# z and six LRU gate projections moved from whole units to seven-product pairs, with the SSD rows, the LRU states and the group norm

## The chip, the cores and the metric

The kernel runs on one core of a Trainium2 chip. It is written by hand for the core's engines: TensorE (PE) multiplies, VectorE (DVE), ScalarE (ACT) and GpSimd (POOL) work on elements, SyncE (SP) issues DMAs; POOL and ACT issue DMAs too. Each engine takes its own instructions in the order of the program and waits on semaphores for the others. The metric is the device time of one execution in microseconds, lower is better; the runs give a median.

## The reference

One decoder layer with 1024 tokens and width 1024 in float32. `xn` is the RMS norm of the input, and one projection of it feeds three mixers and three merge gates. Cut to what matters here:

```
proj = hn @ w_in                                   # u, v | xb, gate | z | x,B,C | dt | g0, g1, g2
yb = gelu(gate) * lru_scan(conv(xb))               # 8 blocks of 128 channels
y  = ssd(conv(x,B,C), dt) + x * d_skip             # 4 groups of 256 channels
y  = y * silu(z)
yg = y.reshape(.., 4 groups, 256)
yc = yg * rsqrt(mean(yg * yg, -1) + EPS) * norm_g  # the group norm
gates  = sigmoid(g + b_gate)
merged = sum over branches: gates[k] * (y_k @ w_branch_k)
h = x + merged @ w_out;  h = h + (relu(rms(h) @ W1) ** 2) @ W2;  out = rms(h)
```

Each product is done to nearly float32 accuracy from a high and a low part of both operands: high x high, high x low, low x high, three matmuls in place of one.

## The kernel before

A matmul is 128 x 128 weights by 512 columns. The program has these stages: the input norm and the projection v (to about 140 us), the **unit stage** (to 770 us), the **pair stage** (to about 1005 us), the branch merge, the output projection, and the MLP.

*Unit stage.* A unit is 128 output channels for all 1024 tokens: 8 slices of the input x 3 x 2 halves of tokens = 48 matmuls (`product`, L555) into a PSUM tile `ps` of which there are two. Then its `post` runs: a conv (L576, L578), a gelu (`gelu2`, L235 to L238) or a gate. `queue` holds the units in order: for each SSD group r B, C, x0, x1, z0, z1, then for two LRU heads the conv input `xb` and the gate; after that eight gMLP units. There are 48 in all: 8 for z, 8 for LRU gates, 16 for the rest of SSD, 8 for `xb`, 8 for gMLP. Work that belongs to finished units stands in generators in `pending`. `step` (after each unit) moves each one on by a `yield`. For SSD these are `ssd_stages`: `s1_` builds decays and C B products, `s2_` the states, `s3_` the rows y (L738 to L740), which it multiplies by the gated z (L741) and squares (L743); `s4_` does the group norm (L749 to L759): a matmul with a matrix of ones sums over the channels, ACT takes the root, and DVE makes and corrects the reciprocal. For an LRU head, `stages` does the two small gate products (L816), the scan (L831) and the product with the gelu gate. Results go to DRAM as `yb_d`, `yc_d`, `ya_d`. In this stage a scheduler sets the order of the engines' rows.

*Pair stage.* A pair is 256 output channels. Instead of 96 matmuls for two units it takes 84: a Strassen-like form with seven products of 12 matmuls each (`seventh`, L478), of sums and differences of blocks of the weights (A11, A12, A22, S1 to S4) and of `xn` (B11, B21, B22, T1 to T4, made once by `x_forms`). Twelve pairs make the three merge gates. The order is written out by hand (`manual_schedule`): p1 of a pair, p4 of the pair before, then p2, p5, p6, p3, p7. Behind each product stands what frees its PSUM tile, and between them the preparation of the next pair's weights: `cast1`, `sums1`, `sums2`, `cast12`, `cast22`, and `cast34` of this pair. A cast is `split`: ACT makes the high part (L132), DVE the low part (L133). p1, p6, p7 and p4 accumulate into one PSUM tile `b1`: p6 waits until ACT has copied what p1 left there (L934), p7 until ACT has copied that of p6 (L950), and p4 until DVE has added that of p7 (L958) to its partner. p5 and p3 share `b2` in the same way (L945, L954).

Of the kernel before, what the change touches and what calls it, by code (L numbers as in the profile page):

```python
# [36 lines left out]
def trunk_kernel(ctx: ExitStack, tc: tile.TileContext, x, norm_mix_g, w_in, b_gate, gmlp_ln_g, gmlp_ln_b,  # L37
# [23 lines left out]
    mixers = ExitStack()  # L61
    halfp = mixers.enter_context(tc.tile_pool(name="half", bufs=16))
    lrup = mixers.enter_context(tc.tile_pool(name="lruw", bufs=1))
    const = mixers.enter_context(tc.tile_pool(name="const", bufs=1))
# [139 lines left out]
    def columns(name, rws, n):  # L204
        ps = aux()
        nc.tensor.transpose(out=ps[:, :n], in_=rws[:n, :P], identity=ident[:n, :n])
        cols = const.tile([P, n], F32, name=name)
        nc.vector.tensor_copy(out=cols, in_=ps[:, :n])
        return cols
# [75 lines left out]
    with tc.manual_schedule():  # L285
# [21 lines left out]
        ones = const.tile([P, P], F32, name="ones")  # L307
# [115 lines left out]
    va = columns("va", acs, P)  # L423
# [157 lines left out]
    gd = [dram.tile([KD, P, T], F32, name=f"g{b}_d") for b in range(3)]  # L581

# [39 lines left out]
    def ssd_units(g):  # L622
        S = {}

        def xbc(key, ct):
            def post(ps):
                c = act()
                conv(c, ps, [scw[:, j * 16 + ct:j * 16 + ct + 1] for j in range(4)], vh[:, SCB + ct:SCB + ct + 1])
                t = act()
                actv(t, c, AF.Tanh)  # L630
                stt(out=c, in0=t, scalar=1.0, in1=c, op0=ALU.add, op1=ALU.mult)
# [5 lines left out]
        def z(j):  # L637
            def post(ps):
                t = act()
                actv(t, ps, AF.Tanh, scale=0.5)  # L640
                stt(out=t, in0=t, scalar=1.0, in1=ps, op0=ALU.add, op1=ALU.mult)
                S["z", j] = t
            unit_in(C_Z + (2 * g + j) * P, post)

        xbc("b", 8 + g)
        xbc("c", 12 + g)
        xbc("x0", 2 * g)
        xbc("x1", 2 * g + 1)
        z(0)
        z(1)  # L650

    def ssd_stages(g, S):
# [3 lines left out]
        xdt, xw, E, cb, pv, er, sq = {}, {}, {}, {}, {}, {}, {}  # L656
# [68 lines left out]
        def s3_(half):  # L725
            tk = hsl(half)
            for j in range(2):
# [9 lines left out]
                Z = S["z", j]  # L737
# [3 lines left out]
                tt(out=Z[:, tk], in0=y, in1=Z[:, tk], op=ALU.mult)  # L741
                sq[half, j] = half_()
                actv(sq[half, j], Z[:, tk], AF.Square)  # L743
            nc.gpsimd.tensor_tensor(out=sq[half, 0], in0=sq[half, 0], in1=sq[half, 1], op=ALU.add)

        def s4_(half):
            tk = hsl(half)
            vs = aux()
            mm(vs, ones, sq[half, 0], start=True, stop=True)  # L749
            r, q = half_(), half_()  # L750
            actv(r, vs, AF.Sqrt, scale=1.0 / 256, bias=eps4)
            nc.vector.reciprocal(out=r, in_=r)  # L752
            tt(out=q, in0=r, in1=r, op=ALU.mult)
            stt(out=q, in0=vs, scalar=256 * 4.0 * EPS, in1=q, op0=ALU.add, op1=ALU.mult)
            ts(out=q, in0=q, scalar1=-0.5 / 256, scalar2=1.5, op0=ALU.mult, op1=ALU.add)
            tt(out=r, in0=r, in1=q, op=ALU.mult)
            for j in range(2):
                Z = S["z", j]
                stt(out=Z[:, tk], in0=Z[:, tk], scalar=va[:, SNG + 2 * g + j:SNG + 2 * g + j + 1], in1=r, op0=ALU.mult, op1=ALU.mult)  # L759
                nc.gpsimd.dma_start(out=yd["c"][2 * g + j][:, tk], in_=Z[:, tk])  # L760

# [10 lines left out]
        s4_(0)  # L772
# [3 lines left out]
        yield  # L776
        s3_(1)
        yield
        yield
        s4_(1)  # L780


    def lru_units(h):
        S = {}

        def post_x(ps):
# [8 lines left out]
            for half in range(2):  # L795
                p_ = half_(dt=F32R), half_(dt=F32R)
                split(p_[0], p_[1], xb[:, hsl(half)])
                S["xs"].append(p_)

        def post_g(ps):  # L800
            S["g2"] = act()
            gelu2(S["g2"], ps, T)
            later(stages())
            if h == 7:
                v_group(0)

        def stages():
# [25 lines left out]
            nc.gpsimd.tensor_tensor(out=S["g2"], in0=y, in1=S["g2"], op=ALU.mult)  # L833
            nc.gpsimd.dma_start(out=yd["b"][h], in_=S["g2"])
            yield

        unit_in(C_XB + h * P, post_x)
        unit_in(C_GATE + h * P, post_g)
# [80 lines left out]
    class GatePair:  # L919
        def __init__(self, br, e):  # L920
            self.br, self.e = br, e
            self.w = Weights(w_in, C_G + br * D + e * P, w4)
# [4 lines left out]
        def gate(self, o, src, b):  # L927
            actv(o, src, AF.Tanh, scale=0.5, bias=vh[:, BG + self.br * 8 + self.e + b:BG + self.br * 8 + self.e + b + 1])

        def p1(self):  # L930
            self.b1 = gps.tile([P, HF], F32, tag="gps", name=nm("gps"))
            self.mul(self.b1, "A11", "B11", True)
            self.o0 = act()
            actv(self.o0[:, hsl(0)], self.b1, AF.Copy)  # L934

        def p2(self):
            b0 = gps.tile([P, HF], F32, tag="gps", name=nm("gps"))
            self.mul(b0, "A12", "B21", True)
            tt(out=self.o0[:, hsl(0)], in0=b0, in1=self.o0[:, hsl(0)], op=ALU.add)

        def p5(self):
            self.b2 = aux()
            self.mul(self.b2, "S1", "T1", True)
            self.o1 = act()
            actv(self.o1[:, hsl(1)], self.b2, AF.Copy)  # L945
            self.gate(self.o0[:, hsl(0)], self.o0[:, hsl(0)], 0)

        def p6(self):
            self.mul(self.b1, "S2", "T2", False)
            actv(self.o0[:, hsl(1)], self.b1, AF.Copy)  # L950

        def p3(self):
            self.mul(self.b2, "S4", "B22", False)
            tt(out=self.o0[:, hsl(1)], in0=self.b2, in1=self.o0[:, hsl(1)], op=ALU.add)  # L954

        def p7(self):
            self.mul(self.b1, "S3", "T3", False)
            tt(out=self.o1[:, hsl(1)], in0=self.b1, in1=self.o1[:, hsl(1)], op=ALU.add)  # L958
            self.gate(self.o0[:, hsl(1)], self.o0[:, hsl(1)], 0)
            nc.gpsimd.dma_start(out=gd[self.br][self.e], in_=self.o0)  # L960

        def p4(self):
            self.mul(self.b1, "A22", "T4", False)
            self.gate(self.o1[:, hsl(0)], self.b1, 1)
            self.gate(self.o1[:, hsl(1)], self.o1[:, hsl(1)], 1)
            nc.gpsimd.dma_start(out=gd[self.br][self.e + 1], in_=self.o1)

    pairs = [(br, e) for br in (1, 0, 2) for e in range(0, KD, 2)]
    cur = []

    def first_pair():
        z = GatePair(*pairs.pop(0))
# [8 lines left out]

    for r in range(4):
        ssd_units(r)
        lru_units(2 * r)
        lru_units(2 * r + 1)
# [39 lines left out]
    two = (P, 2, HF)  # L1025
# [196 lines left out]

    z, prev = cur.pop(), None
    with tc.manual_schedule():
        z.w.cast22()
        while z:
            nxt = GatePair(*pairs.pop(0)) if pairs else None
# [31 lines left out]
            prev, z = z, nxt  # L1259
    for n in list(XF):  # L1260
# [529 lines left out]
```

## Time and profile before

| | us |
|---|---|
| runs, median of 3 | 1985.93 (1985.53 to 1985.93) |
| the profiled execution | 1988.2 |
| its span, first to last instruction | 1986.5 |
| PE / DVE / ACT / POOL busy | 1929.9 / 1340.0 / 988.2 / 313.6 |
| granted PE clock, mean | 0.987 |

The page's costliest groups are matmuls. Its columns are line, engine, operation, output and inputs, shape and count, then busy time and the mean of one in ns, then the idle time of the engine before them and what ended it. Here the two groups of the units and one of the pair stage:

```profile
L555 PE MATMUL ps<-xn,wh 128*128 128x512 f32 x1536 | 418.4, 392 | 0.0
...
L555 PE MATMUL ps<-xn,wl 128*128 128x512 f32 x768 | 236.7, 389 | 0.0
...
L478 PE MATMUL gps<-xn,wt 128*128 128x512 f32 x432 | 102.2, 389 | 2.1 <-DVE a L238 2.1
```

1536 + 768 = 2304 matmuls are the 48 units. The 389 ns are the time through the array; the next matmul starts sooner, so the rate is read from the start times.

### The profile page before, as it was taken

The numbers are of one execution on the slowest core, as the hardware profiler recorded it, in microseconds if no ns is written. First come the engines' busy times: TensorE is split into PE (matmuls) and PEld (weight loads), VectorE is DVE, ScalarE is ACT, GpSimd is POOL, SyncE is SP. The second block draws the span as 40 slices with busy tenths as digits, with TensorE's granted clock in tenths as the row PEclk, the third lists the DMA queues.
The fourth block names the chain that finished last, engine by engine and source line by source line (L and its number), as shares of the span: only waits on it lengthen the run. The fifth ranks groups of instructions, "written<-read, shape, count | busy, mean of one in ns | idle before, by whom it ended". The sixth has DMA issues, their size and how long they took to land.

```text
span 1986.5 us, 23821 instructions
## 1 busy us (share of the span) xinstructions
PE 1929.9 (97%) x9012; PEld 1607.3 (81%) x9012; DVE 1340.0 (67%) x1917; ACT 988.2 (50%) x1431; POOL 313.6 (16%) x406
## 2 busy tenths in 40 slices
PE   8999999999999998999999999998999999999996
PEld 7998878788788787888888888777788887888885
DVE  5485666875866688444477888247665657788787
ACT  6425665756756643444354544166555555243243
POOL 4112222232322443000010110000111110000000
PEclk8999999999999999999999999999999999999998
DMA  4256547457366473333398986331544358543532
GB/s 160 59 147 137 116 106 156 94 117 143 92 133 130 107 191 106 117 117 106 122 277 273 267 219 177 138 106 54 178 156 164 128 184 299 174 154 123 190 115 88
DMA packets 207208, 293.93 MB, mean 148 GB/s; under 512 B 12804, under 2 KB 125652, under 8 KB 207092
## 3 DMA queue, kind: packets, MB, share of 16 engines
q1 hardware_dynamic: 163540, 151.20, 24.7%
q0 software_dynamic: 34544, 119.69, 23.5%
q10 hardware_dynamic: 9008, 21.51, 3.1%
q8 instruction: 71, 1.16, 0.2%
q14 instruction: 45, 0.37, 0.1%
HBM read 188.41 MB, written 67.24 MB: 129 GB/s over the span
## 4 chain that ended last, share of the span: by engine, by line
PE 80%; DVE 11%; ACT 4%; issue 3%; DMA 2%; POOL 1%; SPq 0%; ACTq 0%; DVEq 0%; POOLq 0%
PE aux L478 39%; PE ps L555 22%; PE gps L478 8%; PE aux L257 4%; PE aux L1312 2%; PE aux L816 1%; PE aux L735 1%; PE aux L731 1%; DVE a L578 1%; ACT a L1361 1%; DVE a L831 1%; DVE h L752 1%; DVE rsq_q L111 1%; DVE a L133 1%; DVE a L702 1%
## 5 line engine op out<-in xcount | busy, mean ns | idle before, releaser
L555 PE MATMUL ps<-xn,wh 128*128 128x512 f32 x1536 | 418.4, 392 | 0.0
L555 PEld LDWEIGHTS ps<-xn,wh 128*128 128x128 f32 x1536 | 286.8, 188 | 61.2 <-issue 2.8
L478 PE MATMUL aux<-b,b 128*128 128x512 f32 x1152 | 263.9, 389 | 0.1
L478 PEld LDWEIGHTS aux<-b,b 128*128 128x128 f32 x1152 | 216.1, 188 | 45.3 <-DVE b L133 0.5
L555 PE MATMUL ps<-xn,wl 128*128 128x512 f32 x768 | 236.7, 389 | 0.0
L478 PE MATMUL aux<-a,b 128*128 128x512 f32 x960 | 219.4, 389 | 0.0
L478 PEld LDWEIGHTS aux<-a,b 128*128 128x128 f32 x960 | 180.2, 188 | 37.4
L555 PEld LDWEIGHTS ps<-xn,wl 128*128 128x128 f32 x768 | 144.1, 188 | 30.3
L478 PE MATMUL aux<-b,wt 128*128 128x512 f32 x672 | 156.9, 389 | 0.0
L478 PEld LDWEIGHTS aux<-b,wt 128*128 128x128 f32 x672 | 126.1, 188 | 26.2
L132 ACT ACTIVATE b<-wt 128x1024 fp32r<-128x1024 f32 x88 | 90.7, 1053 | 83.8 <-DMA wt<-u_d 58.8
L133 DVE TENSOR_TENSOR b<-wt,b 128x1024 fp32r<-128x1024 f32 x88 | 107.2, 1219 | 17.3 <-ACT b L132 17.3
L133 DVE TENSOR_TENSOR wt<-a,wt 128x1024 fp32r<-128x1024 f32 x52 | 63.7, 1225 | 73.1 <-ACT wt L132 73.1
L1542 DVE TENSOR_TENSOR a<-aux,a 128x512 f32<-128x512 f32 x112 | 77.0, 688 | 50.5 <-PE aux L478 50.4
L478 PE MATMUL gps<-xn,wt 128*128 128x512 f32 x432 | 102.2, 389 | 2.1 <-DVE a L238 2.1
L526 ACT ACTIVATE wh<-raw 128x1024 fp32r<-128x1024 f32 x48 | 50.7, 1056 | 104.3 <-PE ps L555 99.2
L478 PEld LDWEIGHTS gps<-xn,wt 128*128 128x128 f32 x432 | 80.9, 188 | 19.2 <-issue 2.5
L133 DVE TENSOR_TENSOR a<-a,a 128x1024 fp32r<-128x1024 f32 (+1 forms) x61 | 61.8, 1020 | 38.9 <-ACT a L132 38.8
L478 PE MATMUL aux<-a,wt 128*128 128x512 f32 x336 | 81.6, 400 | 3.4 <-ACT a L1419 3.4
L578 DVE SCALAR_TENSOR_TENSOR a<-ps,scw,a 128x1023 f32<-128x1023 f32 (+2 forms) x48 | 61.1, 1273 | 33.3 <-ACT a L576 32.5
L528 POOL DMA_DIRECT2D wl<-raw x48 | 42.9, 893 | 248.5 <-ACT wl L527 88.3
L478 PEld LDWEIGHTS aux<-a,wt 128*128 128x128 f32 x336 | 65.0, 194 | 18.0 <-ACT a L1419 4.2
(339 smaller groups left out, 3372.2 us busy)
## 6 DMA issues: line engine op xcount, KB each, us to landing
wt<-u_d SPq DMA_DIRECT2D x54, 512.0 KB
raw<-in_w_in_dram SPq DMA_DIRECT2D x48, 512.0 KB
wl<-raw POOLq DMA_DIRECT2D x48, 512.0 KB, 5.0
u_d<-a POOLq DMA_DIRECT2D x48, 512.0 KB, 5.2
g_d<-a POOLq DMA_DIRECT2D x24, 512.0 KB, 2.9
a<-g_d ACTq DMA_DIRECT2D x24, 512.0 KB
rt<-in_w_mlp_up_dram SPq DMA_DIRECT2D x17, 512.0 KB
a<-acs_d POOLq DMA_DIRECT2D x32, 256.0 KB, 8.0
```

The source lines that it names most:

```text
L111: stt(out=q, in0=r, scalar=nh, in1=r, op0=ALU.mult, op1=ALU.mult)
L132: actv(dst_hi, src, AF.Copy)
L133: (eng or nc.vector).tensor_tensor(out=dst_lo, in0=src, in1=dst_hi.bitcast(F32), op=ALU.subtract)
L257: mm(ps[:, :nt], X.tok(a, k, c), wk[k][w], start=(k == 0 and i == 0), stop=(k == KD - 1 and i == 2))
L478: mm(ps, lhs[l][kk], rhs[r][kk], start=(new and n == 0), stop=(n == 11), skip_group_check=not new)
L526: actv(hi, raw, AF.Copy)
L528: nc.gpsimd.dma_start(out=lo, in_=raw, accum_op=ALU.add)
L555: mm(ps[:, hsl(h)], w[wi][:, k, :], a.rhs(ai, k, h), start=(n == 0), stop=(n == 3 * KD - 1))
L578: stt(out=dst[:, j:], in0=ps[:, :T - j], scalar=taps[3 - j], in1=dst[:, j:], op0=ALU.mult, op1=ALU.add)
L702: tt(out=e[:, cc], in0=e[:, cc], in1=cbm[:, i].unsqueeze(1).to_broadcast([P, 4, P]), op=ALU.mult)
L1312: mm(ps, M.tok(a, k, c), wo[nb][k][w], start=(k == 0 and a + w == 0), stop=(k == KD - 1 and a == 1))
L1542: tt(out=h, in0=ps, in1=h, op=ALU.add)
```

## The change

- z (8 blocks) and six of the eight LRU gate blocks leave the unit list: 14 units fewer. They become seven pairs among the twelve gate pairs: kind "z" (4 pairs), "g" (3) and "t" (the gates as before). The heads 6 and 7 keep their gate units.
- The LRU heads are spread 2, 2, 1, 3 over the four SSD groups.
- `s3_` stores its rows y to DRAM (`yr_d`) and is done; `s4_` goes away. Heads 0 to 5 store their states (`hr_d`); their stages start one step later.
- A z or g pair reads the rows back (`rows`, in two halves, from SP) and hands its half to a generator: `post_g` is the gelu and the product, `post_z` the gate, the product, and the whole group norm. The main loop calls `step` seven times per pair.
- The order of the branches among the gate pairs changes, and the two halves of a gate pair are stored by half of the tokens, not by block.
- `ones` and `va` move to the lasting pool; the vectors' pool is closed before the pair stage, and four tiles `actx` take its place.

```diff
@@ ssd_units, ssd_stages
-        z(0)
-        z(1)
...
                 stt(out=y, in0=Xf[j][:, tk], scalar=dcol[:, 2 * g + j:2 * g + j + 1], in1=y, op0=ALU.mult, op1=ALU.add)
-                tt(out=Z[:, tk], in0=y, in1=Z[:, tk], op=ALU.mult)
-                sq[half, j] = half_()
-                actv(sq[half, j], Z[:, tk], AF.Square)
-            nc.gpsimd.tensor_tensor(out=sq[half, 0], in0=sq[half, 0], in1=sq[half, 1], op=ALU.add)
-
-        def s4_(half):
...
+                nc.gpsimd.dma_start(out=yr_d[2 * g + j][:, tk], in_=y)
...
@@ lru_units
+            if h < PLAIN:
+                later(stages(False))
...
+            if gated:
+                nc.gpsimd.tensor_tensor(out=S["g2"], in0=y, in1=S["g2"], op=ALU.mult)
+                nc.gpsimd.dma_start(out=yd["b"][h], in_=S["g2"])
+            else:
+                nc.gpsimd.dma_start(out=hr_d[h], in_=y)
...
-        unit_in(C_GATE + h * P, post_g)
+        if h >= PLAIN:
+            unit_in(C_GATE + h * P, post_g)
...
-    class GatePair:
+    class Pair:
+        def rows(self, half):
+            if self.kind != "t":
+                self.y[half] = actx()
+                nc.sync.dma_start(out=self.y[half], in_=self.part({"z": yr_d, "g": hr_d}[self.kind], half))
+
+        def done(self, half):
+            if self.kind == "t":
+                nc.gpsimd.dma_start(out=self.part(gd[self.br], half), in_=self.o[half])
+            else:
+                later({"z": self.post_z, "g": self.post_g}[self.kind](half))
+
+        def post_g(self, half):
+            o, y, t = self.o[half], self.y[half], actx()
+            actv(t, o, AF.Square)
+            stt(out=t, in0=t, scalar=1.0 / GELU_C, in1=o, op0=ALU.add, op1=ALU.mult)
+            actv(t, t, AF.Tanh, scale=GELU_S * GELU_C)
+            yield
+            stt(out=o, in0=t, scalar=1.0, in1=o, op0=ALU.add, op1=ALU.mult)
+            tt(out=o, in0=o, in1=y, op=ALU.mult)
+            nc.gpsimd.dma_start(out=self.part(yd["b"], half), in_=o)
+
+        def post_z(self, half):
+            o, y, t = self.o[half], self.y[half], actx()
+            actv(t, o, AF.Tanh, scale=0.5)
+            stt(out=o, in0=t, scalar=1.0, in1=o, op0=ALU.add, op1=ALU.mult)
+            tt(out=o, in0=o, in1=y, op=ALU.mult)
+            actv(t, o, AF.Square)
+            yield
+            tt(out=t[:, 0], in0=t[:, 0], in1=t[:, 1], op=ALU.add)
+            yield
+            yield
+            vs = aux()
+            mm(vs, ones, t[:, 0], start=True, stop=True)
+            r, q = y[:, 0], y[:, 1]
+            actv(r, vs, AF.Sqrt, scale=1.0 / 256, bias=eps4)
+            nc.vector.reciprocal(out=r, in_=r)
+            tt(out=q, in0=r, in1=r, op=ALU.mult)
+            stt(out=q, in0=vs, scalar=256 * 4.0 * EPS, in1=q, op0=ALU.add, op1=ALU.mult)
+            ts(out=q, in0=q, scalar1=-0.5 / 256, scalar2=1.5, op0=ALU.mult, op1=ALU.add)
+            tt(out=r, in0=r, in1=q, op=ALU.mult)
+            for b in range(2):
+                col = SNG + self.e + b
+                stt(out=o[:, b], in0=o[:, b], scalar=va[:, col:col + 1], in1=r, op0=ALU.mult, op1=ALU.mult)
+            nc.gpsimd.dma_start(out=self.part(yd["c"], half), in_=o)
...
+    for i in range(3):
+        pairs.insert(5 * i + 1, ("z", 0, 2 * i))
+        pairs.insert(5 * i + 3, ("g", 0, 2 * i))
+    pairs.insert(15, ("z", 0, 6))
...
+    for r, heads in enumerate(((0, 1), (2, 3), (4,), (5, 6, 7))):
...
@@ main loop of the pair stage
             z.p1()
             z.w.cast34()
+            step()
             if prev:
                 prev.p4()
+                step()
             z.p2()
...
+            step()
             z.p5()
...
+            step()
             z.p6()
...
+            step()
             z.p3()
...
+            step()
             z.p7()
...
+            step()
             prev, z = z, nxt
```

The 19 pairs now come in the order t z t g t t z t g t t z t g t z t t t: behind each z and each g pair stands a gate pair.

How the change moves instructions is seen in the order of the built programs. On DVE, before, between the low parts of the next pair's first weights (L133, `wt`) and p7's add (L958) stand the weight sums (L502 to L507), a cast, p3's add (L954) and a cast:

```order
L133 TENSOR_TENSOR wt_6506<-rt_6468,wt_6505 128x1024
L502 TENSOR_TENSOR a_6525<-a_6469 128x512
L503 TENSOR_TENSOR a_6526<-rt_6468,a_6469 128x512
L506 TENSOR_TENSOR a_6525<-a_6525,rt_6468 128x512
L507 TENSOR_TENSOR a_6526<-rt_6468,a_6525 128x512
L133 TENSOR_TENSOR wt_6545<-a_6525,wt_6544 128x1024
L954 TENSOR_TENSOR a_6485<-aux_6509,a_6485 128x512
L133 TENSOR_TENSOR a_6561<-a_6469,a_6561 128x512
L958 TENSOR_TENSOR a_6522<-gps_6472,a_6522 128x512
```

After, in the gate pair behind the first z pair, the same place on DVE begins with that pair's own p2 add (L976) and the low part, and then comes the norm chain of one half (L957 to L964; `x` are the `actx` tiles) and the sum of the other half's squares (L950):

```order
L976 TENSOR_TENSOR a_5733<-gps_5758,a_5733 128x512
L133 TENSOR_TENSOR wt_5773<-rt_5716,wt_5772 128x1024
L957 RECIPROCAL x_5655<-x_5655 128x512
L958 TENSOR_TENSOR x_5655<-x_5655 128x512
L959 SCALAR_TENSOR_TENSOR x_5655<-aux_5776,x_5655 128x512
L960 TENSOR_SCALAR x_5655<-x_5655 128x512
L961 TENSOR_TENSOR x_5655<-x_5655 128x512
L964 SCALAR_TENSOR_TENSOR a_5653<-a_5653,va,x_5655 128x512 x2
L950 TENSOR_TENSOR x_5753<-x_5753 128x512
L502 TENSOR_TENSOR a_5804<-a_5717 128x512
```

A little further on the same engine, behind the cast of S1 and S2 (L133, `wt`), stands the chain of the other half, and behind it p3's add (L992), a cast and p7's add (L996):

```order
L133 TENSOR_TENSOR wt_5824<-a_5804,wt_5823 128x1024
L957 RECIPROCAL x_5709<-x_5709 128x512
L958 TENSOR_TENSOR x_5709<-x_5709 128x512
L959 SCALAR_TENSOR_TENSOR x_5709<-aux_5827,x_5709 128x512
L960 TENSOR_SCALAR x_5709<-x_5709 128x512
L961 TENSOR_TENSOR x_5709<-x_5709 128x512
L964 SCALAR_TENSOR_TENSOR a_5602<-a_5602,va,x_5709 128x512 x2
L992 TENSOR_TENSOR a_5801<-aux_5788,a_5801 128x512
L133 TENSOR_TENSOR a_5851<-a_5717,a_5851 128x512
L996 TENSOR_TENSOR a_5801<-gps_5720,a_5801 128x512
```

So two chains that stood in the unit stage now stand ahead of p7's add of a gate pair. On PE, in the same gate pair, the last matmuls of p6 (into `gps`) were followed at once by those of p3 (into `aux`):

```order
L478 MATMUL gps_6472<-h_6317,wt_6436 128x512
L478 MATMUL gps_6472<-h_6318,wt_6436 128x512
L478 MATMUL gps_6472<-h_6317,wt_6437 128x512
L478 MATMUL aux_6509<-xn_552,wt_6487 128x512
L478 MATMUL aux_6509<-xn_558,wt_6487 128x512
```

and now the sum matmul of one half (L954) stands between them; that of the other half stands in the same way between p2 and p5:

```order
L478 MATMUL gps_5720<-h_5317,wt_5676 128x512
L478 MATMUL gps_5720<-h_5318,wt_5676 128x512
L478 MATMUL gps_5720<-h_5317,wt_5677 128x512
L954 MATMUL aux_5827<-x_5753,ones 128x512
L478 MATMUL aux_5788<-xn_552,wt_5735 128x512
L478 MATMUL aux_5788<-xn_558,wt_5735 128x512
```

Its input `x_5753` is what DVE writes in the row L950 above.

More of the change, by code (lines that the diff above doesn't have):

```diff
@@ L306, in trunk_kernel @@
         make_identity(nc, ident)
-        ones = const.tile([P, P], F32, name="ones")
+        ones = base.tile([P, P], F32, name="ones")
         nc.vector.memset(ones, 1.0)
@@ L802, in post_g, with stages @@
             gelu2(S["g2"], ps, T)
[L803 to L807, printed above, removed]
+            later(stages(True))
+        def stages(gated):
+            if not gated:
+                yield
             xb, w = S["xb"], S["w"]
@@ L924, in mul, with gate @@
         def mul(self, ps, left, right, new):
             seventh(ps, self.w.op[left], XF[right], new)
-        def gate(self, o, src, b):
-            actv(o, src, AF.Tanh, scale=0.5, bias=vh[:, BG + self.br * 8 + self.e + b:BG + self.br * 8 + self.e + b + 1])
+        def gate(self, half, b, src=None):
+            o = self.o[half][:, b]
+            if self.kind == "t":
+                col = BG + self.br * 8 + self.e + b
+                actv(o, o if src is None else src, AF.Tanh, scale=0.5, bias=vh[:, col:col + 1])
+            elif src is not None:
+                actv(o, src, AF.Copy)
@@ L979, in first_pair @@
         z.w.cast12()
-    for r in range(4):
+    for r, heads in enumerate(((0, 1), (2, 3), (4,), (5, 6, 7))):
         ssd_units(r)
-        lru_units(2 * r)
-        lru_units(2 * r + 1)
+        for h in heads:
+            lru_units(h)
     for g in range(8):
@@ L1258, in trunk_kernel @@
                 make(0, 0, 1)
+            step()
             prev, z = z, nxt
+    assert not pending
+    gx.close()
     for n in list(XF):
```

104 lines of the change are left out of this document (46 added, 58 removed).

## The prediction

> **What bounds the kernel now.** I read the busy shares and the chain first, then windows of the two stages that the change touches, then the timeline of one gate pair.
>
> ```profile
> PE 1929.9 (97%) x9012; PEld 1607.3 (81%) x9012; DVE 1340.0 (67%) x1917; ACT 988.2 (50%) x1431; POOL 313.6 (16%) x406
> ...
> PE 80%; DVE 11%; ACT 4%; issue 3%; DMA 2%; POOL 1%; SPq 0%; ACTq 0%; DVEq 0%; POOLq 0%
> ```
>
> The kernel is a stream of matmuls: PE is busy for 97% and is 80% of the chain that ended last. DVE is the next engine. So an edit is worth the PE time that it removes, less what it makes PE wait. The windows of the unit stage (140 to 770 us) and of the pair stage (790 to 1000 us) say how much room there is:
>
> ```profile
> 140.00:770.00 630.00, 624.66 (x3106) 516.22 (x3105) 437.70 (x584) 365.02 (x502) 181.68 (x209) 1.00 0.55 126
> 790.00:1000.00 210.00, 210.00 (x928) 173.82 (x927) 97.07 (x122) 89.37 (x124) 11.71 (x22) 1.00 0.37 120
> ```
>
> The columns are the window, its length, then busy time and instruction count of PE, PEld, DVE, ACT and POOL, the granted clock, DMA share and GB/s. In the pair stage PE never waits and DVE works 97 of 210 us. In the unit stage PE is idle for 5.3 us of 630, and DVE is at 69%. By its share DVE has room in both, but an in-order queue can run late with a share far under one. The timeline of one pair shows the deadlines:
>
> ```profile
> 845.28 1.23 DVE L133 TENSOR_TENSOR wt<-a,wt 128x1024 fp32r<-128x1024 f32 x1 [2.34 <-ACT wt L132]
> 846.23 5.60 PE L478 MATMUL gps<-xn,wt 128*128 128x512 f32 x24
> 846.43 0.69 DVE L954 TENSOR_TENSOR a<-aux,a 128x512 f32<-128x512 f32 x1
> ...
> 849.14 0.69 DVE L958 TENSOR_TENSOR a<-gps,a 128x512 f32<-128x512 f32 x1 [1.43 <-PE gps L478]
> ...
> 851.66 2.88 PE L478 MATMUL gps<-a,a 128*128 128x512 f32 x12
> 851.86 0.60 ACT L934 ACTIVATE a<-gps 128x512 f32<-128x512 f32 x1 [3.99 <-PE gps L478]
> 852.36 1.05 ACT L132 ACTIVATE wt<-a 128x1024 fp32r<-128x1024 f32 x1
> 853.44 1.23 DVE L133 TENSOR_TENSOR wt<-a,wt 128x1024 fp32r<-128x1024 f32 x1 [3.61 <-ACT wt L132]
> ...
> 859.36 0.69 DVE L502 TENSOR_TENSOR a<-a 128x512 f32<-128x512 f32 x1
> 859.97 0.69 DVE L503 TENSOR_TENSOR a<-rt,a 128x512 f32<-128x512 f32 x1
> ...
> 864.32 1.23 DVE L133 TENSOR_TENSOR wt<-a,wt 128x1024 fp32r<-128x1024 f32 x1 [2.35 <-ACT wt L132]
> ```
>
> The same DVE row comes again 19.04 us later: one pair, 84 matmuls, 2.72 us for each product of 12. The rows at 846.23 are p7 and the next pair's p1. p7 ends at 848.95, its add on DVE runs from 849.14 (row L958) to 849.83, and p4, which accumulates into the same PSUM tile, starts at 851.66. **p4 must wait for p7's add, and today that add is 1.8 us early.** The rows also give DVE's spacing when it has work queued: 1.15 us for 1024 columns (845.28 to 846.43), 0.61 for 512 (859.36 to 859.97); an operation that needs the result before it waits for all of it.
>
> **The change, part by part.**
>
> *Matmuls.* One whole unit in the chain:
>
> ```profile
> 601.63 10.89 PE ps L555 x48
> ```
>
> 14 units of 48 matmuls leave, 14 x 10.89 = 152.5 us; 7 pairs come, 7 x 19.04 = 133.3 us. On PE, **-19.2 us**. The eight sums over a group (`ones` matmuls) move with the group norm and count the same.
>
> *Unit stage.* Besides PE's work the group norm leaves it. One norm chain, with its matmul and its square root, reads today:
>
> ```profile
> 225.12 1.02 PE L749 MATMUL aux<-h,ones 128*128 128x512 f32 x2
> 226.11 0.96 PE L816 MATMUL aux<-h,lw 128*128 128x512 f32 x3
> ...
> 227.08 1.28 ACT L751 ACT_TABLE_LOAD   x1
> 228.38 0.69 ACT L751 ACTIVATE h<-aux,eps 128x512 f32<-128x512 f32 x1
> ...
> 231.37 3.35 DVE L752 RECIPROCAL h<-h 128x512 f32<-128x512 f32 x1
> 234.75 0.69 DVE L753 TENSOR_TENSOR h<-h 128x512 f32<-128x512 f32 x1
> 235.47 0.69 DVE L754 SCALAR_TENSOR_TENSOR h<-aux,h 128x512 f32<-128x512 f32 x1
> 236.20 0.43 DVE L755 TENSOR_SCALAR h<-h 128x512 f32<-128x512 f32 x1
> 236.66 0.69 DVE L756 TENSOR_TENSOR h<-h,h 128x512 f32<-128x512 f32 x1
> 237.38 1.41 DVE L759 SCALAR_TENSOR_TENSOR a<-a,va,h 128x512 f32<-128x512 f32 x2
> ```
>
> The sum matmul takes 1.0 us of PE (225.12 to 226.11), table load and root 2.0 of ACT, and **DVE's chain 7.4 us** (231.37 to 238.79), each step waiting for the last. Eight chains leave: 59 us. So DVE in the unit stage falls to at most 379 us in 630 - 152 - 8 = 470, a share of at most 0.81 after 0.69 (the products with z and the gelus leave too). The stage loses PE cover faster than DVE work, but stays under one. PE's waits there now:
>
> ```profile
> PE aux L816 <- ACT h L132: 4.3, 4, 1.1
> PE aux L816 <- DVE h L133: 0.9, 4, 0.2
> ```
>
> Since the plain heads' LRU stage now starts one unit later than its conv, these 5.2 us could go; the closer packing could bring as much. I take 0, between -5 and +10. The stores of rows and states and their loads back (SP, POOL) are 512 KB at a time and asked for ten or more us ahead; with 37% DMA share in the pair stage I take 0.
>
> *z pairs.* This term decides. `post_z` of a z pair runs beside the next pair, always a gate pair, and its steps stand in the same in-order queues as that pair's casts, copies and adds. I walk it from 0 = end of p7 of the z pair. Missing durations are those of the nearest groups, 1.22 and 1.06 us for 1024 columns:
>
> ```profile
> L631 DVE SCALAR_TENSOR_TENSOR a<-a,a 128x1024 f32<-128x1024 f32 x16 | 19.6, 1222 | 10.7 <-ACT a L630 10.7
> L630 ACT ACTIVATE a<-a 128x1024 f32<-128x1024 f32 x16 | 17.0, 1062 | 30.9 <-DVE a L578 15.9 <-issue 12.3 <-DVE lrs L112 2.7
> ```
>
> - DVE: p7's add 0.2 to 0.9. ACT: tanh to 2.0. DVE: gate and product with y to 4.5. ACT: square to 5.6 (it stands waiting, since the square follows the tanh in its queue), copy of p1 to 6.1, cast S3/S4 to 7.0.
> - DVE: low part of S3/S4 to 8.3, sum of the two squares to 8.9. PE was through with p2 at 8.2 and has the first sum matmul next: **0.7 us idle**.
> - ACT: copy of p4, second tanh to 8.6. DVE: gate and product to 11.3. ACT: square to 12.4, cast of the next pair to 13.3, table load and root to 15.2. DVE: that pair's low part to 14.6, then the first chain, 15.2 to 22.6, and only then the second sum of squares, to 23.2.
> - PE: sum, p5, p6 done at 15.3. Its next instruction is the second sum matmul, which needs that sum of squares: **7.9 us idle**. Then sum, p3, p7, p1, to 32.4.
> - DVE: four weight sums to 25.7; ACT casts S1/S2 to 26.1, loads the table, second root to 28.1. DVE: low part to 27.4, second chain 28.1 to 35.5, p3's add, a low part, and p7's add at 37.3. PE's p4 waits from 32.4: **4.9 us idle**.
>
> Without waits p4 would start at 2.72 + 19.04 + two sums of 1.0 = 23.8. It starts at 37.3, so a z pair costs 13.5 us, four **+54 us**. ACT's waits are part of that. The floor is DVE's work alone between the two p7 adds: seven operations of 1.15, eleven of 0.61, two chains of 7.4 = 29.6 us in a gap of 23.6: 6.0 us for each z pair, 24 in all. I take the walk, since each of its waits follows from the order of the queues. Afterwards DVE is back at its old load and nothing is carried on.
>
> *g pairs.* `post_g` has no matmul, no square root and no reciprocal: per half 2 ACT and 3 DVE operations of 1024 columns. The same walk ends p7's add at 22.2 where p4 is due at 21.8: 0.4 us, three times, **+1.4 us**.
>
> *The clock.* Gaps of 7.9 and 4.9 us may lower it. Two gaps of today, the rows behind them and the windows after:
>
> ```profile
> 773.50 2.96 PE L478 MATMUL gps<-xn,wt 128*128 128x512 f32 x12 [2.08 <-DVE a L238]
> 1245.49 0.50 PE L1312 MATMUL aux<-a,b 128*128 128x512 f32 x1 [4.14 <-ACT a L132]
> ...
> 775.00:780.00 5.00, 2.64 (x12) 1.70 (x11) 5.00 (x8) 1.58 (x2) 2.83 (x1) 1.00 0.72 200
> 1245.00:1250.00 5.00, 3.75 (x9) 2.76 (x10) 3.05 (x3) 1.39 (x2) 0.00 (x0) 0.61 0.99 354
> 1250.00:1255.00 5.00, 5.00 (x18) 3.92 (x17) 1.28 (x2) 1.10 (x2) 0.00 (x0) 0.71 0.84 305
> ```
>
> After 2.1 us the clock stayed at 1.00; after 4.1 us it was 0.61 and 0.71 in the next two windows, which hold 27 matmuls where 44 fit; less 1.3 us of waiting, that is some 2.6 us lost. Here the slow matmuls follow the long gap, when PE would only wait for DVE again (p1 ends 4.9 us early), so I charge nothing: the second gap shrinks instead. The Trainium skill ("TensorE: Matmul & The Clock Gate", section "HAM oscillation — how this bites in real kernels") says that PE must not idle for more than about 3.4 us or it goes back to half clock; both gaps above agree with it. By its window of 3.4 us at half clock, a gap would lose an estimated 1.7 us, and two gaps in four z pairs 14 us if none of it were hidden.
>
> **Sum.** -19.2 + 54 + 1.4 = +36 us. The profiled execution took 1988.2 us (span 1986.5, 1.7 around it), the runs 1985.9 in the median, 0.1% less; on the runs' scale 1985.9 + 36 = **2022 us**, own range 2011 to 2032.
>
> **The rivals.**
>
> *Faster: the post work hides.* If DVE and ACT get through `post_z` while PE has its 23.6 us between the two adds, only the matmuls count: 1985.9 - 19.2 = 1967 us. For it: DVE's share in the pair stage, under a half, and a mean of some 75% with the new work (19 pairs of 8.8 us, eight norm chains of 7.4, some 30 operations of 1.15 and 8 of 0.61, in 361 us). Against it: the work stands in one pair of two, 29.6 us of it; it decides at 23.6 us per z pair, and DVE would have to run its rows a fifth closer than today. 0.09.
>
> *Only DVE's floor.* If ACT's part overlaps better than in my walk, 24 us stay: 1985.9 - 19.2 + 24 + 1.4 = 1992 us. Against it: ACT blocks on its own square and on casts that wait for DVE. 0.12, a third of it under the bound of "same".
>
> *The clock on the path.* If the slow matmuls delay the second chain or p4, up to 2.6 us for each of 8 gaps: 2022 + 21 = 2043 us. For it: the gaps are twice as long as the one measured. Against: 4.9 us of slack behind the first. 0.10.
>
> *The unit stage turns DVE bound.* Three of four groups have two or one LRU heads beside the SSD steps and no other unit between; if the convs come late, PE waits for its PSUM tiles. At the upper bound, +10: 2032 us. 0.09.
>
> The forecast has 0.60. From 1991 to 2038 lie the forecast, most of the floor case, the unit-stage case and part of the clock case, over 8 in 10. A difference of 0.2%, about what a measurement of this kernel can tell from no change, is 4 us: faster 0.09, same 0.04, slower 0.87.
>
> **What would show it.** Right: each of four z pairs is followed by PE waits of about 8 us before a sum matmul (for DVE) and 3 to 5 us before p4 (for DVE's add), and the pair stage takes 19 x 19.04 + 8 + 55 = 425 us. The reciprocals run inside those gaps. The unit stage is about 160 us shorter, with PE waits under 10 us. Wrong: no PE gap over 2 us behind a z pair, DVE rows of `post_z` much shorter than their twins of today, or PE waits of over 15 us in the unit stage.

## The result, and the profile after

The changed kernel takes **2040.18 us** (median of 4 runs, 2035.92 to 2041.73) beside 1985.73 us (1984.37 to 1985.93) of the kernel before on the same chip: a ratio of 1.0272, 95% interval 1.0254 to 1.029. It is slower by 54 us. The forecast was 2022 us (36 us slower), with an own range of 2011 to 2032 and over 8 chances in 10 for 1991 to 2038; the result lies above both. The profiled execution is the fastest of the four: 2035.92 us, span 2033.9, mean granted clock 0.976 after 0.987.

The busy shares and the chain of work that ended last, after:

```profile
PE 1927.3 (95%) x8928; PEld 1597.7 (79%) x8928; DVE 1414.1 (70%) x2000; ACT 1005.9 (49%) x1455; POOL 293.6 (14%) x392
...
PE 59%; DVE 15%; ACT 7%; issue 4%; DMA 3%; POOL 0%; SPq 0%; ACTq 0%; DVEq 0%; POOLq 0%
```

There are 84 matmuls fewer, yet PE is busy for only 2.6 us less (slower clock), and its share of the chain falls from 80% to 59%. What PE waited for, in the view of the waits (awaited row; us in total, times, longest):

```profile
PE aux L954 <- DVE x L950: 35.1, 8, 8.0
PE gps L478 <- DVE a L996: 10.8, 7, 3.1
```

Eight waits of a sum matmul (L954) for DVE's sum of squares (L950), and seven of p4 for p7's add (L996): both are the places that the prediction named. The timeline behind the first z pair:

```profile
657.12 5.60 PE L478 MATMUL gps<-xn,wt 128*128 128x512 f32 x24
...
660.04 0.69 DVE L996 TENSOR_TENSOR a<-gps,a 128x512 f32<-128x512 f32 x1 [1.43 <-PE gps L478]
...
668.93 1.10 PE L954 MATMUL aux<-x,ones 128*128 128x512 f32 x2 [0.77 <-DVE x L950]
...
675.32 3.35 DVE L957 RECIPROCAL x<-x 128x512 f32<-128x512 f32 x1 [0.77 <-ACT x L956]
...
682.67 0.68 DVE L950 TENSOR_TENSOR x<-x 128x512 f32<-128x512 f32 x1
...
683.50 2.04 PE L954 MATMUL aux<-x,ones 128*128 128x512 f32 x2 [7.99 <-DVE x L950]
...
684.56 4.94 PE L478 MATMUL aux<-xn,wt 128*128 128x512 f32 x12
...
688.29 3.35 DVE L957 RECIPROCAL x<-x 128x512 f32<-128x512 f32 x1 [0.78 <-ACT x L956]
...
696.85 0.68 DVE L996 TENSOR_TENSOR a<-gps,a 128x512 f32<-128x512 f32 x1
...
697.59 4.60 PE L478 MATMUL gps<-a,a 128*128 128x512 f32 x12 [2.62 <-DVE a L996]
```

The first row is p7 of the z pair and the next pair's p1; p7, its first half, ends at 659.84 (657.12 + 2.72), 0.2 us before its add. The second sum of squares stands behind the whole first chain on DVE (675.32 to 682.67), so PE idles for 7.99 us; the matmuls after that run slow (4.94 us for 12, 2.88 at full clock); p7's add of the next pair stands behind the second chain, and p4 starts at 697.59, 37.75 us after p7. The prediction's walk had 37.3.

By stages, cut at the first matmul of the pair stage and at the first of the branch merge, before and then after:

```profile
768.43 2.98 PE L478 MATMUL gps<-xn,wt 128*128 128x512 f32 x12
...
1001.26 1.07 PE L478 MATMUL aux<-a,a 128*128 128x512 f32 x4
```

```profile
617.07 2.98 PE L478 MATMUL gps<-xn,wt 128*128 128x512 f32 x12
...
1053.06 1.07 PE L478 MATMUL aux<-a,a 128*128 128x512 f32 x4
```

| | before | after | difference | foreseen |
|---|---|---|---|---|
| up to the pair stage | 768.4 | 617.1 | -151.4 | -160.5 (14 units, 8 sums) |
| pair stage | 232.8 | 436.0 | +203.2 | +196.7 (pairs 133.3, sums 8, waits 55.4) |
| the rest | 985.2 | 980.8 | -4.4 | 0 |

The rest has the same work; most of its 4.4 us is one place, where 24 matmuls behind the same wait of 2.6 us took 8.60 us before and 5.74 after. So two terms are off: the unit stage by +9.1 and the pair stage by +6.5. These figures are of the two profiled executions, 47.4 us apart by their spans; the medians are 54 us apart. The profiled execution before took 2.5 us more than its median and the one after 4.3 us less; no trace shows where these 7 us lie.

PE's waits in the unit stage (140 to 617 us), 10.9 us in all where the prediction's view of the kernel before has 5.2:

```profile
PE aux L669 <- DVE h L730: 4.5, 1, 4.5
PE aux L789 <- DVE h L729: 1.9, 3, 0.6
PE aux L703 <- ACT a L576: 1.8, 1, 1.8
PE aux L789 <- DVE h L714: 1.6, 2, 1.3
PE aux L703 <- DVE h L673: 1.1, 1, 1.1
```

The matmuls behind some of them ran slow: the granted clock was 0.94 from 360 to 380 us and 0.83 from 440 to 460 us, 1.00 in all of the stage before. The timeline around the longest wait:

```profile
424.20 0.89 POOL L528 DMA_DIRECT2D wl<-raw  x1 [14.71 <-ACT wl L527]
...
428.69 2.50 POOL L657 DMA_DIRECT2D a<-acs_d  x4
...
436.01 1.28 ACT L690 ACTIVATE a<-a,acs 128x128 f32<-128x128 f32 x4 [2.23 <-DMA a<-acs_d]
...
441.68 1.19 ACT L576 ACTIVATE a<-ps,va 128x1024 f32<-128x1024 f32 x1
...
442.90 1.28 DVE L578 SCALAR_TENSOR_TENSOR a<-ps,va,a 128x1023 f32<-128x1023 f32 x1 [5.58 <-ACT a L576]
444.10 0.68 DVE L730 TENSOR_TENSOR h<-aux,h 128x512 f32<-128x512 f32 x1
...
444.84 1.11 PE L669 MATMUL aux<-ident,a 128*128 128x128 f32 x4 [4.52 <-DVE h L730]
445.60 2.05 PE L555 MATMUL ps<-xn,wh 128*128 128x512 f32 x4
```

Read from below: PE's transposes need a PSUM tile that DVE's add L730 frees; the add stands behind a conv (L578), which waits for ACT's first step (L576); on ACT that stands behind the decays (L690), which wait for rows from DRAM. GpSimd had asked for these rows (L657) behind weight transfers, which wait for ACT (L527). So the wait passes through four in-order queues. Then the clock is low: 2.05 us for four matmuls, 1.07 at full clock.

### The profile page after: what moved, and what is told of

It reads as the page before. It is cut to its first block, busy times and chain, and to the rows that moved or that the text cites. A ratio compares the mean times of both kernels' runs of the same rounds, so it can differ in the third digit from the quotient of the medians.

```text
span 2033.9 us, 23784 instructions
## 1 busy us (share of the span) xinstructions
PE 1927.3 (95%) x8928; PEld 1597.7 (79%) x8928; DVE 1414.1 (70%) x2000; ACT 1005.9 (49%) x1455; POOL 293.6 (14%) x392
## 4 chain that ended last, share of the span: by engine, by line
PE 59%; DVE 15%; ACT 7%; issue 4%; DMA 3%; POOL 0%; SPq 0%; ACTq 0%; DVEq 0%; POOLq 0%
PE aux L478 39%; PE ps L555 8%; PE gps L478 7%; PE aux L1366 2%; DMA a<-acs_d 1%; DVE x L957 1%; ACT wt L132 1%; DVE a L133 1%; ACT a L1415 1%; DVE a L578 1%; PE aux L789 1%; DMA lr<-in_lru_w_i_dram 1%; DVE rsq_q L111 1%; ACT L956 1%; DVE wt L133 1%
## 5 line engine op out<-in xcount | busy, mean ns | idle before, releaser
L555 PE MATMUL ps<-xn,wh 128*128 128x512 f32 x1088 | 296.1, 393 | 0.0
L555 PEld LDWEIGHTS ps<-xn,wh 128*128 128x128 f32 x1088 | 203.6, 189 | 42.1 <-issue 0.5
L555 PE MATMUL ps<-xn,wl 128*128 128x512 f32 x544 | 168.4, 390 | 0.0
L478 PE MATMUL gps<-xn,wt 128*128 128x512 f32 x684 | 163.2, 392 | 2.4 <-DVE a L238 2.4
L478 PEld LDWEIGHTS gps<-xn,wt 128*128 128x128 f32 x684 | 129.4, 189 | 29.9 <-issue 2.8
L133 DVE TENSOR_TENSOR wt<-a,wt 128x1024 fp32r<-128x1024 f32 x66 | 80.9, 1225 | 83.8 <-ACT wt L132 83.8
L555 PEld LDWEIGHTS ps<-xn,wl 128*128 128x128 f32 x544 | 102.4, 188 | 21.6
L133 DVE TENSOR_TENSOR b<-wt,b 128x1024 fp32r<-128x1024 f32 x88 | 107.1, 1218 | 15.5 <-ACT b L132 15.5
L133 DVE TENSOR_TENSOR a<-a,a 128x1024 fp32r<-128x1024 f32 (+1 forms) x68 | 66.6, 986 | 38.9 <-ACT a L132 38.8
L132 ACT ACTIVATE wt<-a 128x1024 fp32r<-128x1024 f32 x66 | 69.6, 1055 | 44.8 <-DVE a L506 44.5
L132 ACT ACTIVATE a<-a 128x1024 fp32r<-128x1024 f32 (+1 forms) x68 | 55.9, 837 | 50.5 <-DVE a L1548 45.2
L133 DVE TENSOR_TENSOR wt<-rt,wt 128x1024 fp32r<-128x1024 f32 x35 | 42.9, 1225 | 53.3 <-ACT wt L132 53.3
```

The source lines that it names most:

```text
L132: actv(dst_hi, src, AF.Copy)
L133: (eng or nc.vector).tensor_tensor(out=dst_lo, in0=src, in1=dst_hi.bitcast(F32), op=ALU.subtract)
L478: mm(ps, lhs[l][kk], rhs[r][kk], start=(new and n == 0), stop=(n == 11), skip_group_check=not new)
L555: mm(ps[:, hsl(h)], w[wi][:, k, :], a.rhs(ai, k, h), start=(n == 0), stop=(n == 3 * KD - 1))
```

## The experiments

Ratios are to the kernel before, on the same chip, with 95% intervals. Theory Q says that the loss in the pair stage is the order of `post_z` in the queues; its rivals are the load of DVE itself, the clock, and the unit stage.

**1. Without the chain.** The kernel leaves out the rows from the root to the corrections.

```diff
-            actv(r, vs, AF.Sqrt, scale=1.0 / 256, bias=eps4)
-            nc.vector.reciprocal(out=r, in_=r)
...
+            r = vs
```

> Left out: the square root, the reciprocal and the four correcting operations of the group norm in post_z (8 chains); the final product takes the sum of squares itself. Sum matmuls, loads and stores stay. Theory Q (the chains stand in DVE's queue ahead of what PE waits for): between two p7 adds DVE then has 17.6 us of work in a gap of 23.6, only the two waits for the sums of squares are left, about 2 us for each z pair after 15.7 now, so 2040 - 4 x 13.7 = about 1985 us. Rival L (PE waits for the rows read back from DRAM, or the sum matmuls themselves hold it up): no change in the gaps, over 2025 us.

Measured 1983.92 us, ratio 0.9992 (0.9983 to 1.0001): the chain carries 56 us of the time. What stays of the waits for sums:

```profile
PE aux L954 <- DVE x L950: 7.5, 8, 1.1
```

(The waits that the expectation puts at 15.7 us for each z pair sum to 11.2 in the views above, 35.1 us at the sums and 9.8 ahead of p4; with the slow matmuls p4 comes 13.95 us late.) The pair stage now takes 385.0 us (617.3 to 1002.3). And even without the chain the kernel is 16 us above 1985.9 - 19.2 + 1.4 = 1968, of which the unit stage has 9.

**2. The same work, later.** Not a row less, only other places among the pair's rows: the square one step behind the gate, the reciprocal and its corrections one behind the root, the last products one behind these.

```diff
@@ post_z
+            yield
             actv(t, o, AF.Square)
...
             actv(r, vs, AF.Sqrt, scale=1.0 / 256, bias=eps4)
+            yield
             nc.vector.reciprocal(out=r, in_=r)
...
+            yield
             tt(out=r, in0=r, in1=q, op=ALU.mult)
```

> Nothing left out: the steps of post_z come later. The square stands a step behind the gate, the sum matmul and the root two steps later, reciprocal and correction in a step of their own, the last products in another. One half's chain then falls before p7's add of the first pair behind z, the other's behind it. Theory Q with its order: DVE has some 22 us of work before the first p7 add and 16 before the next, PE's wait falls from 15.7 to 0 to 3 us for each z pair: 1978 to 1992 us. Rival A (the amount of the work counts, not where it stands): still over 2015 us.

Measured 1991.23 us, ratio 1.0032 (1.002 to 1.0044). **Three `yield`s are worth 49 us.** DVE has the same rows for each z pair, 29.6 us by the prediction's sum, so its load is not what cost them. Behind each z pair one wait for p7's add is left, and how fast p4 then runs differs:

```profile
687.07 3.01 PE L478 MATMUL gps<-a,a 128*128 128x512 f32 x12 [2.88 <-DVE a L999]
...
787.84 4.61 PE L478 MATMUL gps<-a,a 128*128 128x512 f32 x12 [2.88 <-DVE a L999]
```

**3. The g pairs alone.** z units and group norm in the unit stage as before, the three g pairs as in the change.

> Only the LRU part of the change: six gate blocks as three g pairs, LRU states by way of DRAM, heads spread 2, 2, 1, 3; z stays as units with its norm in the unit stage. The sum of the prediction: 6 x 10.89 - 3 x 19.04 = -8.2, and 0 to 1.4 for the g pairs: 1977 to 1979 us. Theory U (leaving units thins PE's cover in the unit stage): part of it is lost there, 1980 to 1985 us.

Measured 1996.41 us, ratio 1.005 (1.0036 to 1.0064): a miss for both. The pair stage is as foreseen (291.9 us, 15 x 19.04 = 285.6 and 6.3), but the unit stage is only 43.9 us shorter for six units of 10.89. It loses 21 us in the profiled execution, which at 1999.59 us is the slowest of its five; the largest wait, 9.0 us, is for PSUM that comes free late behind convs:

```profile
PE ps L555 <- DVE a L578: 9.0, 6, 2.1
```

**4. Heads spread evenly**, `((0, 1), (2, 3), (4, 5), (6, 7))` in the changed kernel.

> The changed kernel with the LRU heads spread 2, 2, 2, 2 over the SSD groups in place of 2, 2, 1, 3. Theory U1 (PE's wait of 4.5 us behind DVE at 445 us, and the slow clock after it, come from the one short group): 5 to 8 us less, 2032 to 2035 us. Rival: the waits only move, 2038 to 2042 us.

Measured 2043.25 us, ratio 1.029 (1.0276 to 1.0304). The rival held: the spread isn't the cause, and the pair stage begins at 621.2 us after 617.1.

**5. Matmuls in the gap.** 24 extra ones ahead of the second sum matmul, behind each z pair, into a tile that nobody reads.

```diff
+            if prev and prev.kind == "z":
+                fill = gps.tile([P, HF], F32, tag="gps", name=nm("gps"))
+                for i in range(2):
+                    seventh(fill, z.w.op["S2"], XF["T2"], i == 0)
             step()
```

> The changed kernel with 24 more matmuls (5.4 us, into a spare PSUM tile that nobody reads) in each gate pair behind a z pair, between p6 and the second sum matmul, where PE otherwise idles for 8 us; the output is unchanged. Theory C (the slow clock behind the long gap costs time, since the second gap does not absorb it): the gap shrinks to 2.6 us, the clock stays up, 1.7 to 3.4 us less for each z pair, 2027 to 2034 us. Rival H (hidden, as in the prediction: PE waits for DVE anyway): 2038 to 2042 us. If PE were not waiting for DVE there, 22 us more.

Measured 2041.06 us, ratio 1.0276 (1.0261 to 1.0292): no gain and no loss, as rival H said. 96 matmuls of some 0.23 us fit into the gaps for nothing, and a clock kept up there buys nothing, since DVE sets the pace: p4 behind the first z pair starts at 697.67 us, where it started at 697.59. The waits only move:

```profile
PE gps L478 <- DVE a L996: 17.2, 7, 4.8
PE aux L954 <- DVE x L950: 13.4, 8, 2.6
```

**6. The z pairs alone**, with the late steps of 2; all LRU gates as units.

> Only the z part, with the later steps of e2_late: all eight LRU gates stay units, no g pairs, LRU heads 2, 2, 2, 2. The sum: 8 x 10.89 - 4 x 19.04 = -11.0, and 4 x 3 to 4.5 us for what e2_late still waits at p4: 1986 to 1992 us if the unit stage loses nothing. Theory U (the gate units are cover for LRU's and SSD's work on DVE and ACT, and taking them away is what costs in the unit stage): PE's waits there stay at or under the 5 us of before, against 15 and more in e2_late, so 1983 to 1989 us. Rival: the z units were the cover, and the unit stage loses 10 us here too: 1993 us and more.

Measured 2008.09 us, ratio 1.0108 (1.0091 to 1.0125). The pair stage starts at 688.8, so the unit stage is 79.6 us shorter for 87.1 + 8; some 15 us lost, so the rival's loss came and Theory U failed. The profiled execution, at 2013.04 us, is the slowest of its four. The largest wait is for ACT this time:

```profile
PE aux L789 <- ACT a L677: 13.3, 4, 4.4
```

**7. Two of `post_z`'s rows on GpSimd**, to relieve DVE (on 2).

```diff
-            tt(out=o, in0=o, in1=y, op=ALU.mult)
+            nc.gpsimd.tensor_tensor(out=o, in0=o, in1=y, op=ALU.mult)
...
-            tt(out=t[:, 0], in0=t[:, 0], in1=t[:, 1], op=ALU.add)
+            nc.gpsimd.tensor_tensor(out=t[:, 0], in0=t[:, 0], in1=t[:, 1], op=ALU.add)
```

> e2_late, with the product with y and the sum of the squares in post_z moved from DVE to GpSimd (3.5 us of DVE for each z pair). Theory Q: what is left of PE's wait before p4 (2.9 us for each z pair in e2_late, and the slow clock behind it) is DVE's remaining backlog, so 8 to 16 us less than e2_late: 1975 to 1983 us. Rival: the backlog is the order around the late root, not the amount: within 3 us of e2_late.

Measured 2002.42 us, ratio 1.0082 (1.0067 to 1.0097), 11 us worse than 2: a miss for both theories. PE's seven waits for p7's add grew from 12.6 us in 2 to 18.7. GpSimd takes twice as long for the row as DVE did, and DVE's row beside it is longer too:

```profile
665.12 2.40 POOL L947 TENSOR_TENSOR a<-a,x 128x1024 f32<-128x1024 f32 x1 [15.03 <-DVE a L946]
...
666.34 2.27 DVE L133 TENSOR_TENSOR wt<-a,wt 128x1024 fp32r<-128x1024 f32 x1 [1.30 <-ACT wt L132]
...
671.53 2.37 POOL L947 TENSOR_TENSOR a<-a,x 128x1024 f32<-128x1024 f32 x1 [1.54 <-DVE a L946]
671.97 3.02 DVE L133 TENSOR_TENSOR wt<-rt,wt 128x1024 fp32r<-128x1024 f32 x1
```

These DVE rows take 1.23 us elsewhere.

**8 to 10. The decay rows from SP, one more step in `post_z`, and both.** 8 is the changed kernel with the rows from DRAM for the decays (L657 and L663) issued by SP; 9 is number 2 with one more `yield` ahead of the last products, so that p7's add stands ahead of them; 10 is 9 with the rows from SP.

> The changed kernel with one edit: the loads of the decay rows in the SSD steps (E and er) are issued by SP instead of GpSimd. Theory Q (the in-order GpSimd queue): these loads stand behind the accumulating weight transfers, which wait for ACT; ACT then waits for the rows, the conv behind them on ACT is late, DVE's rows behind that conv too, and PE waits (4.5 us at the first s3_ add, then slow matmuls). From SP they come in time: that wait goes, the unit stage gets 4 to 7 us shorter, 2033 to 2036 us. Rival T (the stage is merely thin: with 14 units gone some other row is late next): the waits move, 2038 to 2042 us.

> The late-steps version (experiment e2_late, 1991 us) with one more step between the correction of the reciprocal and the last products, so that p7's add stands ahead of the products of the first half. Theory Q (order of the queue decides): in that version p4 waited 2.9 us for p7's add behind each z pair and then ran slow (4.6 us for 12 matmuls instead of 3.0); the 2.05 us of products are now behind the add: wait 0.9 or less, no slow p4, 2 to 3.6 us for each z pair, 1977 to 1984 us. Rival L (DVE is simply late by its load, so something else of the pair is late by the same): 1988 to 1992 us.

> Both edits: late steps with one more step, and the decay rows from SP. If both theories Q hold the gains add: 4 to 7 us under e9_later, 1971 to 1979 us, which would be faster than both kernels. If the unit stage is merely thin, the time of e9_later within 2 us.

8: 2040.69 us, ratio 1.0283 (1.0269 to 1.0297). 9: 1980.65 us, ratio **0.998 (0.9969 to 0.9991)**. 10: 1980.51 us, ratio 0.9978 (0.9969 to 0.9987). Theory Q held in the pair stage (9), where p4 now waits 0.8 us and runs at full clock:

```profile
683.55 0.68 DVE L1000 TENSOR_TENSOR a<-gps,a 128x512 f32<-128x512 f32 x1
...
684.29 3.03 PE L478 MATMUL gps<-a,a 128*128 128x512 f32 x12 [0.83 <-DVE a L1000]
684.87 1.41 DVE L968 SCALAR_TENSOR_TENSOR a<-a,va,x 128x512 f32<-128x512 f32 x2
686.20 3.34 DVE L959 RECIPROCAL x<-x 128x512 f32<-128x512 f32 x1
```

In 8 the rows came no earlier, since on SP they stood behind the weights' loads, so 8 did not try what it was meant to:

```profile
433.72 0.38 SPq L523 DMA_DIRECT2D raw<-in_w_in_dram  x1
...
434.20 1.94 SPq L657 DMA_DIRECT2D a<-acs_d  x4
...
439.54 1.28 ACT L690 ACTIVATE a<-a,acs 128x128 f32<-128x128 f32 x4 [6.45 <-DMA a<-acs_d]
```

**11 and 12. Cover.** Number 9 with gMLP units moved between the SSD groups: two of them, and three.

> Experiment e9_later (1980.65 us) with the first two of the eight gMLP units moved between the SSD groups (one behind the heads 2 and 3, one behind head 4), and what they start (the forms of xn) still eight units ahead of the end. Same work. Theory T (the unit stage lost cover: z and gate units stood between the SSD steps as plain PE work, and without them the steps of two groups stand closer in the in-order queues): a gMLP unit has a light post and gives PE 10.9 us of work at that place, so the PE waits of the stage (some 9 us beyond the arithmetic) get less by 4 to 8 us: 1972 to 1977 us. Rival B (the stage's rows for DVE, ACT and GpSimd are too long as a sum; moving units only moves the waits): 1979 to 1983 us.

> The same with three gMLP units, one behind the heads of each of the first three groups. Theory T: as much as e11_cover or 1 to 3 us more, 1970 to 1977 us. Rival B: 1979 to 1983 us.

1981.73 us, ratio 0.9982 (0.9973 to 0.9991), and 1978.53 us, ratio **0.9966 (0.9954 to 0.9979)**. Two units bring nothing, as Rival B said; three bring some 2 us (the intervals overlap). By stages the unit stage isn't shorter: the pair stage begins at 623.6 us with two units and at 618.2 with three, after 617.0 in 9. The pair stage is, 377.6 us in both after 382.1: the wait for the DVE row L238 ahead of its second product, 2.4 us in 9 with a slow product behind it (4.58 us), is gone there, and one of 3.9 or 3.5 us for that row stands in the unit stage instead. So that the moved units acted as cover isn't shown.

**13 and 14. The decay rows a step earlier**, on 9 and on 12.

```diff
@@ ssd_stages
         rows_in(0)
+        yield
         yield
...
         s1_(0)
         yield
+        rows_in(1)
         s2_(0)
         yield
         s3_(0)
-        rows_in(1)
```

(with the steps started at x0 in place of x1, so that all but the rows stays where it was)

> Experiment e9_later (1980.65 us) with the loads of the decay rows E asked for one step (one unit, 10.9 us) earlier in the SSD steps, for both halves; all else in the same steps. Moving them to SP (e8_rows_sp) had not brought them earlier, so it had not tried this. Theory Q: ACT's wait for these rows holds the conv behind it, the conv holds DVE's add, and PE waits 4.6 us at the transposes (L669), then runs slow; with the rows there in time that goes: 1973 to 1978 us and no wait over 2 us at L669. Rival T (the lateness is general, the next row is late by as much): 1979 to 1983 us, with as much waiting elsewhere in the stage. The rows also take two buffers a step longer; if that holds the weights' way, it is slower than 1983 us.

> The same edit on e11_cover3 (1978.53 us). Theory Q: its wait of 4.6 us at L703 hangs on the same rows or not at all; where it does, 1971 to 1976 us. Rival T: 1976 to 1981 us.

1981.25 us, ratio 0.9982 (0.9973 to 0.999), and 1997.66 us, ratio 1.0061 (1.0047 to 1.0074). In 13 the longest wait at the transposes falls from 4.6 to 1.5 us, and another grows:

```profile
PE aux L790 <- DVE h L713: 8.6, 3, 3.5
```

So at this place the late rows were one link, and the stage is as long without it (617.4 us after 617.0), as Rival T said. In all, ACT still waits 26.0 us for such rows after 21.1 in 9, so what the stage would take with every row in time isn't shown. In 14 the same edit costs 19 us, all of it in the unit stage (the pair stage begins at 639.9 us after 618.2); whether that is by the two buffers that the rows now hold a step longer was not tried.

## Why the direction was right and the size wrong

- *PE's arithmetic, -19.2 us.* Right: 84 matmuls fewer, and what is left of the pair stage in experiment 9 is 382.1 us (617.0 to 999.1), 12 above 19 pairs and eight sums.
- *z pairs, 13.5 us each.* The mechanism was right at each of its waits: 0.7, 7.9 and 4.9 us foreseen, 0.77, 7.99 and, with PE slower in between, 2.62 measured. p4 starts 37.75 us after p7 behind all four, where the walk had 37.3, so 13.95 us each. Experiment 2 shows that it is the order: the same rows elsewhere give 49 us back.
- *The clock, charged at nothing.* Half right. Behind the 7.99 us gap the slow matmuls only fill the wait for the second chain, as the step said (experiment 5). But behind the shorter gap ahead of p4 the clock can be low too: p4 took 4.60 and 4.47 us behind gaps of 2.62 and 3.07, and 3.02 and 3.03 behind 1.86 and 2.20. With the slow second product of the stage (4.58 us, 2.96 before) that is some 5 us. These and 0.45 for each of the four walks make up the 6.5 us of the pair stage.
- *g pairs, +1.4 us.* Right: 0.34 or 0.35 us at each of three.
- *The floor of 6.0 us for each z pair.* It was none: it took all of `post_z` to lie between two p7 adds. Experiment 9 puts the last products and a reciprocal behind the second add, into the pair that follows, and lies at 1980.65 us, under the 1992 of that rival.
- ***The unit stage, taken as 0 between -5 and +10.*** **This step failed**: it lost 9.1 us in the profiled execution, the largest part of the miss. I had weighed DVE's share (0.81 at most; measured 343.8 of 475 us, 0.72) and named the right danger, an in-order queue that runs late with a share far under one, but took the middle. In its place the runs show PE waits of 10.9 us instead of 5.2, where the prediction expected under 10, and slow matmuls behind them; the longest wait passes through GpSimd, ACT and DVE. What makes these queues late stays open. The loss doesn't follow the number of units taken away: 9 us for all 14, 21 for the six gates alone, 15 for the eight z alone (the last two in executions 3 and 5 us above their medians). Moving heads, queues or rows (4, 8, 13) moves the wait and leaves the stage at 617.4 to 621.2 us. That plain units between the SSD steps had covered for late queues is a guess, which 11 and 12 did not show.
- *The range.* The unit stage's +10 and the clock stood as rivals, each added alone to 2022, and both came. The profiled executions give 36.2 + 9.1 + 6.5 - 4.4 = 47.4 us, and the medians 54. Small terms bounded on the same side should have been added: with +10 and the clock's 21 the upper end is 2053 us.

The change's idea holds, its schedule doesn't: with the steps of 9 and the units of 12, the same pairs are 0.34% faster than the kernel before (0.21 to 0.46%), of the 19.2 us that the arithmetic offers some 7.

## What to carry to other kernels

When work moves beside an in-order stream, walk its rows through the queues between two deadlines: a load that fits by its sum (29.6 us a z pair, no bound in experiment 9) cost 60 us by its places (2040.18 to 1980.65), and steps of a long chain belong behind the adds that free PSUM. When units leave a stage whose other engines run in-order chains, charge it at the unfavourable bound: the change lost 9 us there, its two halves alone (3 and 6) 21 and 15. Before a row goes to GpSimd to relieve DVE, look at what a DVE row takes beside it.

## What the runs showed of the hardware

- *The clock after short gaps.* The same product, the second of the pair stage, in the timelines of experiment 8 and of experiment 10:

```profile
624.27 2.99 PE L478 MATMUL gps<-xn,wt 128*128 128x512 f32 x12 [2.10 <-DVE a L238]
```

```profile
623.94 4.58 PE L478 MATMUL gps<-xn,wt 128*128 128x512 f32 x12 [2.10 <-DVE a L238]
```

  After 2.10 us of waiting, 12 matmuls took 2.99 us (granted clock 1.00) and 4.58 us (0.58); after 2.88 us, 3.01 (1.00) and 4.61 (0.66) within one execution (experiment 2). So a gap of 2 to 3 us may or may not lower the clock, for some 1.6 us. The prediction's two gaps, 2.1 us without and 4.1 with effect, looked like a threshold between them, and so agreed with the Trainium skill's 3.4 us ("TensorE: Matmul & The Clock Gate", section "HAM oscillation — how this bites in real kernels"); the runs here don't.
- *DVE beside GpSimd.* In experiment 7 a DVE row with two inputs took 2.27 and 3.02 us beside GpSimd products of 2.40 and 2.37 us, 1.23 without. The Trainium skill ("GPSIMD Engine Reference", section "1. Specifications") names this: the two engines share their way to SBUF, and DVE rows with two SBUF inputs contend. In these two cases it is DVE that loses: GpSimd's product of that shape takes no less in the kernel before (L833, 2.41 us in the median), and both DVE rows end 1.09 us after GpSimd's (668.61 after 667.52, 674.99 after 673.90), as if they had stood until it was done.
